# Hybrid encoder with experts: six pairs of split tiles with a set lead, splits ahead of all other work, and down rows in groups of four, four and three

## The chip, the cores and the metric

The kernel runs on one core of a Trainium2 chip. The metric is the device time of one launch in microseconds (us); the comparison is between the kernel before and the kernel with the change.

## What is computed

Two pre-RMSNorm residual layers on 256 tokens of width 1024, then a final RMSNorm, all in float32. Layer 0 is a bidirectional gated linear attention mixer and a dense SwiGLU; layer 1 is a banded attention with ALiBi and sinks, and then eight SwiGLU experts of which each token uses two. The part that the change is mostly about is

```
def swiglu(h, w_gate, w_up, w_down):
    return (silu(h @ w_gate) * (h @ w_up)) @ w_down      # 1024 -> 2816 -> 1024

logits = t @ router;  top_val, top_idx = top_k(logits, 2);  top_w = softmax(top_val)
for e in range(8):
    out += combine[:, e:e+1] * swiglu(t, w_gate[e], w_up[e], w_down[e])
```

The weights of one expert are 3 x 1024 x 2816 floats, 34.6 MB; the eight experts have 277 MB of the 341 MB that the kernel reads.

## The kernel before, in words

**Splits.** Products are made to near-float32 precision on float32r operands: each operand is the sum of a high part (rounded to float32r) and a low part. For a weight tile, ScalarE (ACT) writes `hi = copy(raw)` (line 174) and VectorE (DVE) writes `lo = raw - hi` (line 175). With both operands split a product takes three matmuls (`mm3`, lines 221 to 223: high with high, high with low, low with high). An expert of *kind 3* works so, on up to 128 gathered tokens. An expert of *kind 2* holds at most 64 tokens, so the high and the low part of the tokens sit side by side in the 128 columns of one operand, and two matmuls do (lines 1157 and 1158: one with `hi`, one with `lo` of the weights). The eight experts run in the order kind 3, 2, 3, 2, 3, 2, 3, 2; those after the first are sorted by token count, so that their weights are addressed by a register.

**The weight stream.** One object, `Weights`, carries all weights of the kernel in one list. `pump` starts loads into free raw slots from the SP queue; `split` makes the next `hi` and `lo` pair; `take` splits until `ahead` pairs beyond the one wanted are there and hands over one. Before the change a raw slot is 3072 floats a partition, one load fills it, and it is split as two tiles of up to 1536 floats; a slot is free when its second tile has been split. There are four raw slots at first, six after the first mixer and seven in the expert layer. The pairs come from a pool of three, and `ahead` is 1.

**As it is.** Of each kind 2 expert, four of the 48 tiles are not split (`AS_IS`, loads 1, 13, 17 and 20, the second half of each): TensorE (PE) takes the raw float32 tile itself (line 1155).

**One expert.** Gate and up each go in two halves of 11 column chunks; a half is eight tiles of 128 rows x 1408 columns, spread over three PSUM banks of 512, 512 and 384 columns (`UP` = 4, 4 and 3 chunks). After the eighth tile the banks are taken out (kind 2: ACT copies; kind 3: ACT Silu for gate, a DVE product for up). `turn_over` turns three such groups at a time to `hth` (and `htl`), hidden units on partitions, in the gate steps of the second half and at the first three down steps. Down goes in eight steps of three chunks of 128 rows (the last of one), each a pair of tiles of 512 columns, into two banks. At the fourth down step of a kind 3 expert the tokens of the next two experts are gathered (`after`, lines 1092 to 1116). The four `put` products of an expert, with their DVE additions to `h` (line 1230), run in the up steps of the next one.

**Order.** The program text gives a rank, and a list scheduler with a timeline model puts each engine's instructions into one queue; each engine runs its queue in order and waits at semaphores.

Of the kernel before, what the change touches and what calls it, by code (L numbers as in the profile page):

```python
# [11 lines left out]
F32 = mybir.dt.float32  # L12
# [6 lines left out]
P = 128  # L19
# [18 lines left out]
NQ = 16  # L38
# [13 lines left out]
WIDE = (3, 3, 3, 3, 3, 3, 3, 1)  # L52
# [8 lines left out]
AS_IS = (1, 13, 17, 20)  # L61
# [7 lines left out]
RAW = 3072  # L69
N_A, N_B, N_C = 4, 2, 1  # L70
# [8 lines left out]
def by_rows(w, r0, n, c0, c1, cut):  # L79

    return (w, r0, n, c0, c1), [(slice(k, min(k + cut, n)), slice(0, c1 - c0)) for k in range(0, n, cut)]


def by_cols(w, r0, n, c0, cuts):

    at = [sum(cuts[:i]) for i in range(len(cuts) + 1)]
    return (w, r0, n, c0, c0 + at[-1]), [(slice(0, n), slice(i, j)) for i, j in zip(at, at[1:])]


def plan_columns(w, c0, n=4):  # L90

    return [by_rows(w, k * P, n, c0, c0 + 512, 2) for k in range(0, KC, n)]


def plan_down(wd, c, cuts):

    loads = []
    f = 0
    for i in range(0, len(cuts), 2):
        n = sum(cuts[i : i + 2])  # L100
        loads.append(by_rows(wd, f * P, n, c * HALF, (c + 1) * HALF, cuts[i]))
        f += n
    return loads


def plan_dense(wg, wu, wd):


    loads = []
    f0 = 0  # L110
    for n_f in BLOCKS:
        for w in (wg, wu):
            for k in range(0, KC, 4):
                loads.append(by_cols(w, k * P, 4, f0 * P, (3 * P, (n_f - 3) * P)))
        f0 += n_f
    return loads + plan_down(wd, 0, DOWN[0]) + plan_down(wd, 1, DOWN[0])


def plan_expert(wg, wu, wd, last=False):


    loads = []
    for f0 in (0, FH):
        for w in (wg, wu):
            loads += [by_rows(w, k * P, 2, f0 * P, (f0 + FH) * P, 1) for k in range(0, KC, 2)]
    if last:
        return loads + plan_down(wd, 0, DOWN[0]) + plan_down(wd, 1, DOWN[1])
    f = 0
    for n in WIDE:
        loads.append(by_cols(wd, f * P, n, 0, (HALF, HALF)))  # L130
        f += n
    return loads


class Weights:
# [3 lines left out]

    def __init__(self, nc, split_pool, plan, slots, ahead=1, as_is=()):  # L140
        self.as_is, self.used = as_is, None
        self.nc, self.pool, self.plan, self.slots, self.ahead = nc, split_pool, plan, deque(slots), ahead
        self.loaded = deque()
        self.ready = deque()
        self.next = 0
        self.pump()

    def pump(self):
        while self.slots and self.next < len(self.plan):
            (w, *at), cuts = self.plan[self.next]  # L150
            src = rows(w if isinstance(w, bass.AP) else w(), *at)
            slot = self.slots.popleft()
            raw = slot.tile([P, RAW], F32, name="raw")
            v = self.view(raw, src.shape[1], src.shape[2])
            self.nc.sync.dma_start(v, src)
            for i, (a, b) in enumerate(cuts):
                as_is = (self.next, i) in self.as_is
                self.loaded.append((v[:, a, b], slot if i == len(cuts) - 1 else None, as_is))
            self.next += 1

    def view(self, t, n1, n2):
        return t[:, : n1 * n2].rearrange("p (a b) -> p a b", a=n1)

    def split(self):
        nc = self.nc
        v, slot, as_is = self.loaded.popleft()
        if as_is:
            self.ready.append((v, None))
            self.used = slot
            return  # L170
        n1, n2 = v.shape[1], v.shape[2]
        hi = self.view(self.pool.tile([P, SUB], F32R, name="hi"), n1, n2)
        lo = self.view(self.pool.tile([P, SUB], F32R, name="lo"), n1, n2)
        nc.scalar.activation(hi, v, AF.Copy)  # L174
        nc.vector.tensor_sub(lo, v, hi.bitcast(F32))  # L175
        self.ready.append((hi, lo))
        self.free(slot)

    def free(self, slot):
        if slot:  # L180
            self.slots.append(slot)
            self.pump()

    def done(self):

        slot, self.used = self.used, None
        self.free(slot)
# [5 lines left out]
    def take(self, n1, n2):  # L193
# [3 lines left out]
        assert list(wh.shape[1:]) == [n1, n2], (wh.shape, n1, n2)  # L197
        return wh, wl


@with_exitstack
def hybrid_encoder(ctx: ExitStack, tc: tile.TileContext, a: dict, out: bass.AP):
# [43 lines left out]
    for c0 in (0, KW, 2 * KW, 2 * KW + 512, 2 * KW + VW, 2 * KW + VW + 512):  # L246
        plan += plan_columns(w_in, c0, 4 if c0 else 2)
# [3 lines left out]
    plan += [by_rows(w_qkv, 0, KC, c0, c0 + 256, 4) for c0 in range(0, NQ * HD, 256)]  # L251
# [18 lines left out]
    as_is = set()  # L270
    for s in range(1, NE):
        if KINDS[s] == 2:
            as_is |= {(len(plan) + i, 1) for i in AS_IS}
        plan += plan_expert(*[expert_weights(n, s) for n in moe_w], s == NE - 1)
    weights = Weights(nc, split_p, plan, [raw_a] * 2, as_is=as_is)
# [752 lines left out]
    def moe_layer(x, cst):  # L1028
        with tc.tile_pool(name="moe", bufs=1) as g:
# [109 lines left out]
            def expert(src, kind, xe, weight, between=None, late=(), last=None):  # L1139
# [11 lines left out]
                def mm(ps, ah, al, bh, bl, start, stop):  # L1151
                    if kind == 3:
                        mm3(ps, ah, al, bh, bl, start, stop)
                    elif bl is None:
                        nc.tensor.matmul(ps, lhsT=ah.bitcast(F32), rhs=bh, start=start, stop=stop)  # L1155
# [30 lines left out]
                for f0 in (0, FH):  # L1186
                    ga = g.tile([P, FH * P], F32, name="gate")
                    up_ = g.tile([P, FH * P], F32, name="up") if kind == 2 else None
                    for m in ("g", "u"):
                        banks = [mm_bank() for _ in UP]  # L1190
                        for k in range(KC):
                            wh, wl = src.take(1, FH * P)
                            for (c, n), b in zip(UP, banks):
                                cs = slice(c * P, (c + n) * P)
                                b = b[:, : n * P]
                                mm(b, chunk(xeh, k), chunk(xel, k), wh[:, 0, cs], wl and wl[:, 0, cs], k == 0, k == KC - 1)
                                if k < KC - 1:
                                    continue
                                if kind == 2:
                                    nc.scalar.copy((ga if m == "g" else up_)[:, cs], b)  # L1200
                                elif m == "g":
                                    nc.scalar.activation(ga[:, cs], b, AF.Silu, scale=back[1])
                                else:
                                    nc.vector.tensor_mul(ga[:, cs], ga[:, cs], b)
                                if m == "u":
                                    todo.append((c, n, f0 + c, ga, up_))
                            if not wl:
                                src.done()
                            if not back:
                                back.extend(rest())  # L1210
                            elif todo and m == "g" and k in (1, 3, 5):
                                turn_over(*todo.popleft())
                            elif late and m == "u" and k in (1, 3, 5, 6):
                                late.popleft()()
# [34 lines left out]

                def down(c, b, f, n):  # L1250
                    wh, wl = src.take(n, HALF)
                    for j in range(n):
                        mm(b, chunk(hth, f + j), chunk(htl, f + j), wh[:, j, :], wl and wl[:, j, :], f + j == 0, f + j == FC - 1)
                    if not wl:
                        src.done()
# [16 lines left out]
                f = 0  # L1272
                for n in WIDE:
# [5 lines left out]
                    f += n  # L1279
# [82 lines left out]
            with tc.If(n_most > CAP):  # L1362
                with tc.For_i(0, NE, 1) as e:
# [6 lines left out]
                    puts, _ = expert(Weights(nc, split_p, plan_expert(*w), [raw_a] * N_A), 3, xe[0], wt)  # L1370
# [50 lines left out]
    raw_b = ctx.enter_context(tc.tile_pool(name="raw_b", bufs=N_B))  # L1421
    weights.slots += [raw_b] * N_B
    weights.pump()
# [5 lines left out]
    raw_c = ctx.enter_context(tc.tile_pool(name="raw_c", bufs=N_C))  # L1429
    weights.slots += [raw_c] * N_C  # L1430
    weights.pump()
# [32 lines left out]
```

## Time and profile before

| | |
|---|---|
| three runs | 1230.92, 1230.09, 1230.82 us, median 1230.82 us |
| profiled execution | 1229.29 us, its span 1227.5 us, mean granted PE clock 0.985 |
| busy in the span | PE 1162.9, PEld (weight loads of PE) 984.9, DVE 967.3, ACT 817.8, POOL 94.4 us |
| `lo` on DVE (line 175) | 469 instructions, 728.9 us |
| `hi` on ACT (line 174) | 469 instructions, 619.5 us |
| read from HBM | 341.19 MB |

Busy times are sums of recorded durations. Matmuls overlap, so a PE that is busy all the time isn't at its peak; the chain of waits shows how far apart their ends are. In time the span is: the first mixer to about 143 us, dense SwiGLU to about 340 us, attention to about 440 us, routing to about 461 us, then the experts, whose stages on PE begin at 560.78 us (kind 2), 644.2 (3), 747.93 (2), 832.5 (3), 935.92 (2), 1020.52 (3) and 1123.74 us (2, the last).

### The profile page before, as it was taken

The page shows a single profiled execution, that of the slowest core. Times are in us where ns is not written, and L with a number is a line of the kernel's source. Part 1 is how long each engine was busy: PE and PEld are TensorE (multiplying, and loading weights), DVE is VectorE, ACT ScalarE, POOL GpSimd, SP SyncE. Part 2 cuts the span into 40 slices and gives each one's busy share as a digit, 9 for nine tenths or more (in the row PEclk, how much of TensorE's full clock was granted, in tenths as well). Part 3 has the DMA queues.
Part 4 walks back from the last instruction along what each step waited for, and adds up shares of the span by engine and source line. Part 5 has one row for each costly group of instructions (what it writes and reads, how often), then busy time and mean ns, then how long its engine had stood idle before and what let it go on. Part 6 is the DMA issues. An engine that isn't in the chain of part 4 may idle for free.

```text
span 1227.5 us, 17018 instructions
## 1 busy us (share of the span) xinstructions
PE 1162.9 (95%) x6384; PEld 984.9 (80%) x6384; DVE 967.3 (79%) x1120; ACT 817.8 (67%) x982; POOL 94.4 (8%) x248
## 2 busy tenths in 40 slices
PE   7989999999988989999999999999999999999994
PEld 7879899998888778887878887877887877887872
DVE  5786765564488667898989888988988988987986
ACT  4653544444468647777877777877777877776874
POOL 2000200000058320000000000000000000000003
PEclk9999999999999979999999999999999999999998
DMA  8342764554442147989999988999988999998981
GB/s 281 119 157 86 269 222 151 191 201 158 132 170 96 61 176 271 365 309 344 422 405 393 362 310 326 422 384 400 365 323 313 422 396 406 349 358 292 412 333 37
DMA packets 95281, 343.41 MB, mean 280 GB/s; under 512 B 6404, under 2 KB 10678, under 8 KB 95192
## 3 DMA queue, kind: packets, MB, share of 16 engines
q1 hardware_dynamic: 92400, 340.81, 74.0%
q10 hardware_dynamic: 2648, 0.92, 0.3%
q8 instruction: 52, 0.85, 0.3%
q0 software_dynamic: 144, 0.52, 0.1%
q14 instruction: 37, 0.30, 0.1%
HBM read 341.19 MB, written 1.05 MB: 279 GB/s over the span
## 4 chain that ended last, share of the span: by engine, by line
PE 75%; DVE 11%; ACT 6%; issue 4%; DMA 2%; POOL 2%; ACTq 0%; DVEq 0%; POOLq 0%
PE mm L222 17%; PE mm L223 16%; PE mm L221 16%; DVE lo L175 7%; PE mm L1158 7%; PE mm L1157 6%; PE mm L1155 3%; PE tr L1176 3%; ACT hi L174 3%; PE mm L1224 1%; PE tr L1105 1%; DMA sink_raw<-in_swa_sinks_dram 1%; ACT p L900 1%; DVE y L1248 1%; PE tr L1167 1%
## 5 line engine op out<-in xcount | busy, mean ns | idle before, releaser
L175 DVE TENSOR_TENSOR lo<-raw,hi 128x1408 fp32r<-128x1408 f32 (+2 forms) x469 | 728.9, 1582 | 165.5 <-ACT hi L174 163.9
L174 ACT ACTIVATE hi<-raw 128x1408 fp32r<-128x1408 f32 (+2 forms) x469 | 619.5, 1342 | 304.8 <-PE mm L223 168.5
L221 PE MATMUL mm<-xh,hi 128*128 128x256 f32 x560 | 156.3, 286 | 4.8 <-ACT hi L174 3.8
L222 PE MATMUL mm<-xl,hi 128*128 128x256 f32 x560 | 157.8, 285 | 0.9 <-DVE xl L374 0.9
L223 PE MATMUL mm<-xh,lo 128*128 128x256 f32 x560 | 156.1, 284 | 0.0
L222 PE MATMUL mm<-lo,xeh 128*128 128x512 f32 (+1 forms) x384 | 145.4, 379 | 3.8 <-DVE lo L175 3.6
L223 PE MATMUL mm<-hi,xel 128*128 128x512 f32 (+1 forms) x384 | 144.0, 375 | 0.0
L221 PEld LDWEIGHTS mm<-xh,hi 128*128 128x128 f32 x560 | 105.9, 192 | 6.6 <-ACT hi L174 4.9
L1158 PE MATMUL mm<-lo,xeh 128*128 128x512 f32 x360 | 100.5, 389 | 9.7 <-DVE lo L175 9.6
L222 PEld LDWEIGHTS mm<-xl,hi 128*128 128x128 f32 x560 | 106.6, 191 | 1.5 <-DVE xl L374 1.1
L222 PE MATMUL mm<-lo,hth 128*128 128x512 f32 x264 | 105.0, 398 | 2.2 <-DVE lo L175 2.2
L223 PEld LDWEIGHTS mm<-xh,lo 128*128 128x128 f32 x560 | 105.9, 191 | 0.5 <-issue 0.3
L223 PE MATMUL mm<-hi,htl 128*128 128x512 f32 x264 | 104.4, 395 | 0.0
L221 PE MATMUL mm<-hi,hth 128*128 128x512 f32 x264 | 104.3, 401 | 0.0
L221 PE MATMUL mm<-hi,xeh 128*128 128x512 f32 (+1 forms) x384 | 103.8, 377 | 0.1
L1157 PE MATMUL mm<-hi,xeh 128*128 128x512 f32 x360 | 98.7, 385 | 1.0 <-ACT hi L174 0.8
L222 PEld LDWEIGHTS mm<-lo,xeh 128*128 128x128 f32 x384 | 72.5, 189 | 22.4 <-DVE lo L175 7.2
L1158 PEld LDWEIGHTS mm<-lo,xeh 128*128 128x128 f32 x360 | 63.2, 188 | 29.7 <-DVE lo L175 20.9
L223 PEld LDWEIGHTS mm<-hi,xel 128*128 128x128 f32 x384 | 72.4, 189 | 11.4
L1157 PEld LDWEIGHTS mm<-hi,xeh 128*128 128x128 f32 x360 | 65.9, 188 | 15.1 <-ACT hi L174 3.1
L221 PEld LDWEIGHTS mm<-hi,xeh 128*128 128x128 f32 x384 | 70.5, 189 | 7.6 <-ACT hi L174 1.5
L1158 PE MATMUL mm<-lo,hth 128*128 128x512 f32 x152 | 61.2, 411 | 3.3 <-DVE lo L175 3.2
(305 smaller groups left out, 1557.1 us busy)
## 6 DMA issues: line engine op xcount, KB each, us to landing
raw<-in_moe_w_gate_dram SPq DMA_DIRECT2D x64, 1408.0 KB, 8.7
raw<-in_moe_w_up_dram SPq DMA_DIRECT2D x64, 1408.0 KB, 8.6
raw<-in_moe_w_down_dram SPq DMA_DIRECT2D x53, 1536.0 KB, 9.4
raw<-in_gla_in_proj_dram SPq DMA_DIRECT2D x10, 1024.0 KB, 5.1
raw<-in_dense_w_gate_dram SPq DMA_DIRECT2D x4, 1536.0 KB, 6.6
raw<-in_dense_w_up_dram SPq DMA_DIRECT2D x4, 1536.0 KB, 9.5
raw<-in_dense_w_down_dram SPq DMA_DIRECT2D x4, 1536.0 KB, 7.4
raw<-in_swa_qkv_proj_dram SPq DMA_DIRECT2D x6, 1024.0 KB, 4.8
```

The lines of the kernel that those rows point to most:

```text
L174: nc.scalar.activation(hi, v, AF.Copy)
L175: nc.vector.tensor_sub(lo, v, hi.bitcast(F32))
L221: nc.tensor.matmul(ps, lhsT=ah, rhs=bh, start=start, stop=False)
L222: nc.tensor.matmul(ps, lhsT=ah, rhs=bl, start=False, stop=False)
L223: nc.tensor.matmul(ps, lhsT=al, rhs=bh, start=False, stop=stop)
L900: nc.scalar.activation(p[:, t, :], p[:, t, :], AF.Exp, scale=float(SLOPES[hd]), bias=m[:, 2 + t : 3 + t], accum_out=den[:, t : t + 1])
L1105: i = nc.tensor.matmul(o, lhsT=part[:, t, cs], rhs=oh[:, t, :w], start=t == 0 and part is x.hh, stop=t == NT - 1 and part is x.hl)
L1155: nc.tensor.matmul(ps, lhsT=ah.bitcast(F32), rhs=bh, start=start, stop=stop)
L1157: nc.tensor.matmul(ps, lhsT=ah, rhs=bh, start=start, stop=False)
L1158: nc.tensor.matmul(ps, lhsT=ah, rhs=bl, start=False, stop=stop)
L1167: nc.tensor.transpose(pt[:, i * P : (i + 1) * P], ga[:, (c + i) * P : (c + i + 1) * P], ident)
L1176: nc.tensor.matmul(pt[:, o : o + FEW], lhsT=src_[:, (c + i) * P : (c + i + 1) * P], rhs=by, start=True, stop=True)
```

## The change

- A raw slot is 1536 floats a partition, one load fills it with one tile. There are eight slots all along; the pools `raw_b` and `raw_c` are gone. In the expert layer the slots hold 8 x 6 KB a partition, before 7 x 12 KB.
- From the expert layer on the pairs come in turn from two pools of three, six pairs in all.
- No tile is used as it is; all 48 of a kind 2 expert are split.
- `ahead` is set from a table at every step: it goes 2, 2, 3, 4, 5 through the five parts of a kind 3 expert and 5, 4, 3, 3, 2 through those of a kind 2 expert.
- All ACT and DVE instructions of a gate, up or down step other than splits (taking out the banks, `turn_over`, gather, `put`) are queued behind the last `hi` and the last `lo` that had been issued when the step began (`behind`). The down steps of the last expert have no such order.
- Down of all experts but the last: six groups of 4, 4, 3, 4, 4, 3 row chunks. In a group of n chunks partition p holds rows p*n to p*n+n-1, one run of n*4 KB in memory, cut into tiles of 1536 (for n = 4 the last has 1024); before, a row chunk was 128 rows, one on each partition. To fit, the gate and up banks are read with a step of n floats (`b.rearrange("p (q j) -> p j q")`). `turn_over` still comes at the end of the first three groups, the gather at the end of the fourth.
- Outside the experts the loads are cut to single tiles too (dense gate and up 384 columns a row instead of 768).

```
+AHEAD = {
+    (3, 0, "g"): 2, (3, 0, "u"): 2, (3, FH, "g"): 3, (3, FH, "u"): 4, (3, "d"): 5,
+    (2, 0, "g"): 5, (2, 0, "u"): 4, (2, FH, "g"): 3, (2, FH, "u"): 3, (2, "d"): 2,
+}
-RAW = 3072
-N_A, N_B, N_C = 4, 2, 1
+N_A = 8
...
+def in_a_row(w, r0, n, c0, c1):
+    return w, lambda v: v[r0 : r0 + n * P, :].rearrange("(p r) c -> p (r c)", r=n)[:, c0:c1]
...
+def down_steps():
+    f = 0
+    for _ in range(2):
+        for _, n in UP:
+            for c in range(0, n * D, SUB):
+                yield f, n, c, min(c + SUB, n * D)
+            f += n
...
     def split(self):
-        v, slot, as_is = self.loaded.popleft()
-        if as_is:
-            self.ready.append((v, None))
-            self.used = slot
-            return
...
+        pool = self.pools[self.n_split % len(self.pools)]
+        self.n_split += 1
+        hi = self.view(pool.tile([P, SUB], F32R, name="hi"), v)
+        lo = self.view(pool.tile([P, SUB], F32R, name="lo"), v)
+        i = nc.scalar.activation(hi, v, AF.Copy)
+        j = nc.vector.tensor_sub(lo, v, hi.bitcast(F32))
+        self.last = i.ins, j.ins
         self.ready.append((hi, lo))
-        self.free(slot)
+        self.slots.append(slot)
+        self.pump()
...
+    @contextmanager
+    def behind(self, tc):
+        with ExitStack() as order:
+            for i in self.last:
+                order.enter_context(tc.issue_after(i))
+            yield
...
                         for k in range(KC):
+                            src.ahead = AHEAD[kind, f0, m]
                             wh, wl = src.take(1, FH * P)
...
+                            with src.behind(tc):
+                                for (c, n), b in zip(UP, banks):
...
+                                    to = (ga if m == "g" or kind == 3 else up_)[:, cs]
+                                    if not last:
+                                        to = to.rearrange("p (j q) -> p j q", j=n)
+                                        b = b.rearrange("p (q j) -> p j q", j=n)
...
-                for n in WIDE:
-                    for c, b in enumerate(banks):
-                        down(c, b, f, n)
-                        if f + n == FC:
-                            done(c, b)
-                    mid(0)
-                    f += n
+                for f0, n, c0, c1 in down_steps():
+                    wh, wl = src.take(c1 - c0)
+                    with src.behind(tc):
+                        for i in range(c0, c1, HALF):
+                            f, c = f0 + i // D, i // HALF % 2
+                            ws = slice(i - c0, i - c0 + HALF)
+                            mm(banks[c], chunk(hth, f), chunk(htl, f), wh[:, ws], wl[:, ws], f == 0, f == FC - 1)
+                            if f == FC - 1:
+                                done(c, banks[c])
+                        if c1 == n * D:
+                            mid(0)
...
-    raw_c = ctx.enter_context(tc.tile_pool(name="raw_c", bufs=N_C))
-    weights.slots += [raw_c] * N_C
-    weights.pump()
+    weights.pools = [split_p, ctx.enter_context(tc.tile_pool(name="split_b", bufs=3))]
+    weights.n_split = 0
```

## Rows read from the trace of the kernel before

**Rows 1.** Busy time of each engine over the span (the page's first part).

```profile
PE 1162.9 (95%) x6384; PEld 984.9 (80%) x6384; DVE 967.3 (79%) x1120; ACT 817.8 (67%) x982; POOL 94.4 (8%) x248
```

**Rows 2.** Busy time by stretch: stages of kind 2, kind 2 and kind 3.

```profile
core 0: us, PE busy (x) PEld busy (x) DVE busy (x) ACT busy (x) POOL busy (x), PEclk, DMA share, GB/s
560.78:644.20 83.42, 80.92 (x383) 63.40 (x384) 76.56 (x68) 67.81 (x72) 0.00 (x0) 1.00 0.98 397
...
747.93:832.50 84.57, 81.59 (x383) 62.98 (x383) 76.68 (x68) 67.81 (x72) 0.00 (x0) 1.00 0.98 389
832.50:935.92 103.42, 101.42 (x490) 85.21 (x489) 90.06 (x85) 75.48 (x72) 0.00 (x0) 1.00 0.92 351
```

**Rows 3.** The same view for line 175 (`lo`) alone: DVE busy and count.

```profile
747.93:832.50 84.57, 68.72 (x45) 1.00 0.98 389
832.50:935.92 103.42, 76.52 (x49) 1.00 0.92 351
```

**Rows 4.** Waits, 747.93 to 832.5 us: total us, times, longest.

```profile
ACT hi L174 <- PE mm L1157: 11.7, 9, 2.5
DVE lo L175 <- ACT hi L174: 9.6, 8, 2.1
```

**Rows 5.** Waits, 832.5 to 935.92 us.

```profile
ACT hi L174 <- PE mm L223: 24.2, 34, 1.8
DVE lo L175 <- ACT hi L174: 12.2, 17, 2.2
```

**Rows 6.** Chain of waits, 745 to 790 us: start, us, what.

```profile
754.76 2.36 PE mm L1155 x6
...
761.00 1.28 PE mm L1157 x6
...
769.48 0.93 PE mm L1224 x4
...
783.91 1.28 PE tr L1176 x12
```

**Rows 7.** Chain of waits, 806 to 846 us.

```profile
809.39 2.57 PE mm L1155 x6
...
811.97 0.23 PE mm L1157
...
841.86 0.64 PE mm L221 x3
```

**Rows 8.** Chain of waits, 895 to 925 us.

```profile
909.26 1.76 PE tr L1105 x16
```

**Rows 9.** Timeline of DVE in two kind 2 stretches: start, us, instruction.

```profile
752.19 6.22 DVE L175 TENSOR_TENSOR lo<-raw,hi 128x1408 fp32r<-128x1408 f32 x4
...
818.43 6.76 DVE L175 TENSOR_TENSOR lo<-raw,hi 128x1536 fp32r<-128x1536 f32 x4
```

**Rows 10.** Timeline of PE where a kind 2 expert begins.

```profile
747.93 0.91 PE L1157 MATMUL mm<-hi,xeh 128*128 128x512 f32 x3 [0.30 <-ACT hi L174]
749.59 0.91 PE L1158 MATMUL mm<-lo,xeh 128*128 128x512 f32 x3 [0.75 <-DVE lo L175]
```

**Rows 11.** DVE groups by form, 832.5 to 935.92 us.

```profile
L1204 DVE TENSOR_TENSOR gate<-gate,mm 128x512 f32<-128x512 f32 x4 | 2.6, 681 | 1.8 <-PE mm L223 1.8
```

**Rows 12.** ACT groups by form, 747.93 to 832.5 us.

```profile
L1200 ACT COPY up<-mm 128x512 f32<-128x512 f32 x4 | 2.2, 590 | 1.0 <-PE mm L1158 1.0
```

**Rows 13.** DMA, 760 to 800 us: totals, and issues with median us to landing.

```profile
DMA packets 3563, 16.89 MB, mean 422 GB/s; under 512 B 176, under 2 KB 176, under 8 KB 3560
...
raw<-in_moe_w_up_dram SPq DMA_DIRECT2D x4, 1408.0 KB, 9.0
```

**Rows 14.** Issue times on SP, 760 to 790 us: ns min, median, max.

```profile
L155 SPq DMA_DIRECT2D raw<-in_moe_w_up_dram x4: 372/372/373, 767.7 to 778.9; - x4
```

**Rows 15.** Busy time by stretch: the start and the middle of dense gate and up.

```profile
140.00:160.00 20.00, 17.68 (x134) 16.53 (x134) 14.27 (x25) 9.48 (x16) 10.09 (x86) 1.00 0.92 342
200.00:220.00 20.00, 20.00 (x170) 20.00 (x170) 11.98 (x13) 7.72 (x9) 0.00 (x0) 1.00 0.53 186
```

More of the change, by code (lines that the diff above doesn't have):

```diff
@@ L76, in rows, with chunks, plan_columns @@
     return w[r0 : r0 + n * P, c0:c1].rearrange("(k p) c -> p k c", p=P)
[L79 to L92, printed above, removed]
-def plan_down(wd, c, cuts):
[L97 to L101, printed above, removed]
-        f += n
-    return loads
+def chunks(w, r0, n, c0, c1):
+    return w, lambda v: rows(v, r0, n, c0, c1)
+def in_a_row(w, r0, n, c0, c1):
+    return w, lambda v: v[r0 : r0 + n * P, :].rearrange("(p r) c -> p (r c)", r=n)[:, c0:c1]
+def plan_columns(w, c0):
+    return [chunks(w, k * P, 2, c0, c0 + 512) for k in range(0, KC, 2)]
+def plan_down(wd, c, cuts):
+    at = [sum(cuts[:i]) for i in range(len(cuts))]
+    return [chunks(wd, f * P, n, c * HALF, (c + 1) * HALF) for f, n in zip(at, cuts)]
 def plan_dense(wg, wu, wd):
@@ L113, in plan_dense @@
             for k in range(0, KC, 4):
-                loads.append(by_cols(w, k * P, 4, f0 * P, (3 * P, (n_f - 3) * P)))
+                for c in range(0, n_f, 3):
+                    loads.append(chunks(w, k * P, 4, (f0 + c) * P, (f0 + min(c + 3, n_f)) * P))
         f0 += n_f
     return loads + plan_down(wd, 0, DOWN[0]) + plan_down(wd, 1, DOWN[0])
+def down_steps():
[5 more added lines that the diff above has]
+            f += n
 def plan_expert(wg, wu, wd, last=False):
@@ L124, in plan_expert, with __init__ @@
         for w in (wg, wu):
[L125 removed]
+            loads += [chunks(w, k * P, 1, f0 * P, (f0 + FH) * P) for k in range(KC)]
     if last:
         return loads + plan_down(wd, 0, DOWN[0]) + plan_down(wd, 1, DOWN[1])
[L128 to L132 removed]
+    return loads + [in_a_row(wd, f * P, n, c0, c1) for f, n, c0, c1 in down_steps()]
 class Weights:
[L140 to L142 removed]
+    def __init__(self, nc, split_pools, plan, slots, ahead=1):
+        self.nc, self.pools, self.plan, self.slots, self.ahead = nc, split_pools, plan, deque(slots), ahead
         self.loaded = deque()
         self.ready = deque()
[L145 removed]
+        self.next = self.n_split = 0
         self.pump()
@@ L149, in pump, with view @@
         while self.slots and self.next < len(self.plan):
-            (w, *at), cuts = self.plan[self.next]
-            src = rows(w if isinstance(w, bass.AP) else w(), *at)
+            w, pick = self.plan[self.next]
+            src = pick(w if isinstance(w, bass.AP) else w())
             slot = self.slots.popleft()
-            raw = slot.tile([P, RAW], F32, name="raw")
-            v = self.view(raw, src.shape[1], src.shape[2])
+            raw = slot.tile([P, SUB], F32, name="raw")
+            v = self.view(raw, src)
             self.nc.sync.dma_start(v, src)
-            for i, (a, b) in enumerate(cuts):
-                as_is = (self.next, i) in self.as_is
-                self.loaded.append((v[:, a, b], slot if i == len(cuts) - 1 else None, as_is))
+            self.loaded.append((v, slot))
             self.next += 1
-    def view(self, t, n1, n2):
+    def view(self, t, like):
+        if len(like.shape) == 2:
+            return t[:, : like.shape[1]]
+        n1, n2 = like.shape[1], like.shape[2]
         return t[:, : n1 * n2].rearrange("p (a b) -> p a b", a=n1)
@@ L165, in split @@
         nc = self.nc
-        v, slot, as_is = self.loaded.popleft()
-        if as_is:
-            self.ready.append((v, None))
-            self.used = slot
-            return
[L171 to L175, printed above, removed]
-        self.ready.append((hi, lo))
-        self.free(slot)
[L179 to L187, printed above, removed]
+        v, slot = self.loaded.popleft()
+        pool = self.pools[self.n_split % len(self.pools)]
[5 more added lines that the diff above has]
+        self.last = i.ins, j.ins
+        self.ready.append((hi, lo))
+        self.slots.append(slot)
+        self.pump()
     def fill(self, n):
@@ L250, in hybrid_encoder @@
     plan += plan_columns(w_qkv, NQ * HD)
-    plan += [by_rows(w_qkv, 0, KC, c0, c0 + 256, 4) for c0 in range(0, NQ * HD, 256)]
+    plan += [chunks(w_qkv, k * P, 4, c0, c0 + 256) for c0 in range(0, NQ * HD, 256) for k in (0, 4)]
     plan += plan_columns(w_so, 0) + plan_columns(w_so, HALF)
@@ L1248, in done @@
                     nc.vector.tensor_sub(y[0][:, c, 1], bank, y[0][:, c, 0].bitcast(F32))
+                src.ahead = AHEAD[kind, "d"]
                 def down(c, b, f, n):
@@ L1252, in down @@
                     for j in range(n):
[L1253 to L1255 removed]
+                        mm(b, chunk(hth, f + j), chunk(htl, f + j), wh[:, j, :], wl[:, j, :], f + j == 0, f + j == FC - 1)
                 if last:
```

66 lines of the change are left out of this document (25 added, 41 removed).

## The prediction

> **What bounds the kernel now.** I read the engine totals first [rows 1]: PE is busy 95% of the span, but matmul records overlap, so this says little; VectorE at 79% is an average over unlike stages. So the next view is busy time by stretch, cut where PE goes from one expert to the next [rows 2]. A kind 2 stage takes 84.57 us and VectorE is busy for 76.68 of them; a kind 3 stage takes 103.42 us, VectorE 90.06. Nearly all of that is `lo` [rows 3]. The first kind 2 stage, 83.42 us with VectorE busy 76.56, repeats the pattern.
>
> What PE itself needs comes from the chain of waits, where successive starts give the real pitch. A kind 2 gate or up tile is six matmuls in 1.28 us, a kind 3 tile three times 0.64 = 1.92, a 512 column down product 0.23, a `put` product 0.23, one turning product 1.28 / 12 = 0.107, a tile taken as it is 2.36 (gate, up) or 2.57 us (down) [rows 6, 7]. Kind 2 before: 30 x 1.28 + 2 x 2.36 + 76 x 0.23 + 2 x 2.57 + 88 x 0.107 + 8 x 0.23 = 77.0 us, so PE loses 7.6 of 84.6. Kind 3: 32 x 1.92 + 132 x 0.23 + 22 x 0.107 + 2 x 1.76 for the gather [rows 8] + 1.9 = 99.6, so it loses 3.8 of 103.4. So kind 3 is bound by PE, and kind 2 has two engines within 8 us of its length.
>
> Why VectorE idles 7.9 us in a kind 2 stage: `lo` waits for `hi`, and `hi` waits for PE to free one of three pairs [rows 4]. In kind 3 the same chain makes most of 13.4 us of idle time (`lo` waits 17 times for `hi`, `hi` 34 times for PE) [rows 5]: there VectorE could run ahead, and has no pair to write. So a kind 2 expert starts with no lead: PE waits 0.75 us for the very first `lo` [rows 10].
>
> **The change part by part.**
>
> *No tile as it is.* Each kind 2 expert gets four more splits. Back to back a `lo` of 1408 takes 6.22 / 4 = 1.56 us, one of 1536 6.76 / 4 = 1.69 [rows 9]: 2 x 1.56 + 2 x 1.69 = 6.5 us more on VectorE, 83.2 us a stage. ScalarE gets fewer than 6 us more on 67.81, and has the room. PE gives back 4.5 us: 32 x 1.28 + 88 x 0.23 + 9.4 + 1.9 = 72.5 us. Taken alone this makes kind 2 a VectorE stage that is only 1.4 us shorter than now with no idle time at all.
>
> *Six pairs and the lead.* A lead of L tiles at the start of a kind 2 stage takes 1.56 L us off VectorE's work there and puts it into the kind 3 stage before. The table allows L = 5, now L is 0. Kind 3 has 13.4 us for it; 5 tiles take 7.8, and then 97.9 of about 102 us are busy. I take L = 4, because the gather and its products fall into the last down steps and compete for VectorE there. Kind 2 then needs 83.2 - 6.2 = 77.0 us of VectorE, above PE's 72.5. The idle part of 7.9 us, mostly waits for a pair, should shrink with six pairs; I take 2.8, with 0 and 7.9 as ends. Kind 2: 79.8 us, that is 4.8 less. By the ends: 75.4 (L = 5, no idle) to 91.1 (L = 0, idle as now).
>
> *Kind 3.* Of the 3.8 us that PE loses, the wait at the end of the stage goes (there is a lead now), the waits of the first tiles stay, since a kind 2 stage still ends with VectorE last. I take 1.5 us less; ends 0 and 3.8.
>
> *Splits ahead of everything else.* Taking out banks, `turn_over`, gather and `put` now stand behind up to five splits on both engines. Where PE is late (kind 3) these splits are done early and nobody waits. Where VectorE is late (kind 2), a `put` addition or a `turn_over` product comes up to four splits, 6.2 us, later. The queue behind is more splits, so VectorE doesn't idle, and PE, which has 72.5 us of work in some 80, can lose it; the first down step that needs a late group comes 4 to 5 steps after its `turn_over`. I take 0; the ends are in the idle range above. The gather moves from after 12 of 22 row chunks to after 15, which leaves 7 x 6 x 0.23 = 9.7 us of down products for it (before 13.8) and its own 3.5; its VectorE work is small next to the five splits beside it. Cost 0, up to 3 us if its last products come late.
>
> *Loads.* The same bytes in twice as many transfers. Issuing takes 0.37 us on SP [rows 14], against some 1.8 us a tile. Now about 9.0 us from issue to landing at 422 GB/s are 3.8 MB, 2.6 transfers of 1.44 MB, in flight [rows 13]; that is 5.3 of the new ones, and eight slots leave 2.7 tiles that wait raw, beside the pairs. At the forecast a pair of experts (69.2 MB) takes 181.7 us, 381 GB/s, under the 422 that the queue has shown over 40 us. I take 0; for the other end see the rivals. Down runs get longer (6 KB, before 4 KB), also 0. On the Trainium skill: "DMA: Bandwidth & Descriptors" (Bandwidth, Measured) wants 1 MiB a transfer for 75% of peak, and these are under it; by its 2 us of fixed time and 436 GB/s one 0.72 MB transfer alone would run at an estimated 198 GB/s and the experts would take twice as long. The trace shows several in flight at once, which hides that fixed time, so I don't use it as a term.
>
> *Banks read with a step.* No row has such a read. Bounds: as now, or twice as long. Kind 3 has six DVE products of about 0.62 us (512 columns 0.68 in [rows 11]), kind 2 twelve ACT copies of about 0.55 (0.59 in [rows 12]): at most 3.8 us more DVE a kind 3 stage and 6.6 ACT a kind 2 stage. ACT has that room; on DVE it would eat into the lead. I take 0, as for the reads in rows. The Trainium skill ("PSUM — Partial Sum Buffer", Specifications) speaks against it: PSUM lines are 8 bytes and a pattern that isn't contiguous slows matmuls; it says nothing of reads by the other two engines, and no run here shows it.
>
> *Before the experts.* Dense gate and up keep PE busy in every microsecond at 186 GB/s [rows 15], so smaller slots and shorter runs have cover; if it went, the 2.3 us that PE is idle at 140 to 160 us show the size. There is less loaded in advance when the experts begin (8 tiles, before 14), but the first expert is kind 3. I take 0, ends -3 and +3.
>
> **Sum.** Four kind 2 stages x 4.8 + three kind 3 stages after one of kind 2 x 1.5 = 23.7 us; the first kind 3 stage is as long as PE needs already. Span 1227.5 - 23.7 = 1203.8, execution 1205.6 (1.8 us lie outside the span), and as the median of runs is 1.5 us above the profiled execution, 1207 us.
>
> **The rivals.**
>
> 1. *VectorE follows without idling.* L = 5, no idle time in kind 2 (75.4 us, -9.2) and kind 3 at PE's 99.6 plus 1.3 (-2.5): 4 x 9.2 + 3 x 2.5 = 44, 1187 us. For it: stretches of [rows 9] already run back to back. Against: two engines at over 95% at once, one fed by the other.
> 2. *The lead isn't built, so the four splits are paid (slower).* A kind 2 stage is 83.2 - 1.56 L + idle; it is longer than 84.6 when L is under (idle - 1.4) / 1.56: at 5 us of idle time, under 2.3. With L = 1 and 5 idle it is 86.6, +2.0 x 4 = 8: 1239 us; with L = 0 and idle as now +26: 1257. For it: evictions and gather in kind 3 now stand in VectorE's queue and wait there for PE, and idle time in bits of at most 2.2 us [rows 5] may not be usable. Against: those bits are waits for a pair, and now there are pairs.
> 3. *Loads bound it.* With 2.7 tiles in store (4.7 us) each hiccup of VectorE leaves the DMA without slots. If a pair then gets only the 351 GB/s of a kind 3 stage now, it takes 197 us, 9 more than now, x 4: 1267 us. For it: in kind 2 the DMA share is 0.98 [rows 2]. Against: in kind 3 it is low because slots come late, not because transfers are slow. By the skill's 1 MiB rule this would be the likely one.
> 4. *Reads with a step cost double.* The lead loses 3.8 us: kind 2 gains 1.0 instead of 4.8, so 15 us of the 24 go: 1222 us. The skill's PSUM sentence would make this one.
> 5. *It cancels.* Lead and idle time gain just what the splits cost: 1231 us.
>
> **How the numbers follow.** What a measurement of this kernel tells from no change is about 0.2%, 2.5 us. Forecast (1195 to 1219) 0.50; rival 1 (below) 0.17; rival 4 0.07; rival 5 0.08; rival 2 0.12; rival 3 0.06. Faster 0.50 + 0.17 + 0.07 = 0.74, same 0.08, slower 0.18. The range takes in rival 1 to its value and rival 2 nearly to its first: 1187 to 1237, leaving out some 7% below and 11% above.
>
> **What would show it.** Per expert 48 `lo` instead of 44 in kind 2, no line for raw tiles in matmuls; kind 2 stages near 80 us with VectorE busy at least 76 and the waits of `hi` for PE smaller; kind 3 stages near 102 us with VectorE busy over 95; no wait of PE for the first `lo` of a kind 2 expert. DMA about 381 GB/s over the experts. The forecast is wrong if kind 2 stages stay above 84 us, if ScalarE's `hi` starts to wait for loads, if the products at the banks last longer than the rows here, or if a kind 3 stage gets longer than 103 us.

## The result, and the profile after

The changed kernel takes 1216.72 us (median of 4 runs, 1213.25 to 1219.08), the kernel before 1230.57 us on the same chip: ratio 0.9883, 95% interval 0.9864 to 0.9902, or 13.9 us less. The forecast was 1207 us: right in sign and inside its range, and 9.7 us too low. The profiled execution has a span of 1215.4 us (before 1227.5).

Line numbers moved: `hi` is line 172, `lo` 173, kind 2 products are 1150 and 1151, the gather's products 1100, its evictions 1107 (ACT) and 1111 (DVE), bank evictions 1200 to 1204. The engine totals of after, which answer to [rows 1]:

```profile
PE 1151.2 (95%) x6384; PEld 994.5 (82%) x6384; DVE 982.8 (81%) x1136; ACT 830.1 (68%) x1000; POOL 95.0 (8%) x248
```

PE's busy time fell by 11.7 us, VectorE's rose by 15.5, with sixteen more splits (`lo` is now x485). Busy time by stage of after (kind 2, 3, 2, 3, and the last kind 2 stage to the end of the span), as in [rows 2]: window, length, then busy us and count of PE, PEld, DVE, ACT and POOL, granted clock, DMA share, GB/s.

```profile
562.70:643.04 80.34, 78.12 (x406) 65.57 (x404) 78.94 (x77) 70.13 (x78) 0.00 (x0) 1.00 0.99 386
643.04:742.12 99.08, 98.44 (x467) 83.17 (x466) 89.41 (x77) 72.17 (x67) 0.00 (x0) 1.00 1.00 392
742.12:826.80 84.68, 80.85 (x404) 66.70 (x405) 81.57 (x80) 73.30 (x81) 0.00 (x0) 0.98 0.94 361
826.80:925.90 99.10, 98.44 (x468) 83.16 (x466) 89.43 (x77) 72.22 (x67) 0.00 (x0) 1.00 0.99 391
...
1109.27:1215.40 106.13, 84.93 (x406) 67.41 (x406) 89.75 (x94) 76.34 (x94) 8.79 (x4) 0.91 0.72 267
```

Kind 3 lost 4.3 us (103.4 to 99.1), where 1.5 were forecast. Kind 2 lost nothing (84.57 to 84.68), where 4.8 were forecast; only the first kind 2 stage is at 80.3. A pair of stages (742.12 to 925.90) takes 183.78 us, VectorE busy for 171.0, so 12.8 idle; before it was 188.0 and 166.7, so 21.3 idle. On the span the 12.1 us are made up so: the experts reach their first kind 2 stage 1.9 us later, the three pairs give 7.7, 4.2 and 4.5, and the last stage takes 2.4 more (103.76 before).

The same view for `lo` alone, as in [rows 3], and then for the gather's DVE products (line 1111) and its PE products (line 1100) in the kind 2 stage:

```profile
742.12:826.80 84.68, 72.18 (x46) 0.98 0.94 361
826.80:925.90 99.10, 78.60 (x51) 1.00 0.99 391
```

```profile
742.12:826.80 84.68, 3.65 (x14) 0.98 0.94 361
```

```profile
742.12:826.80 84.68, 3.03 (x16) 2.82 (x16) 0.98 0.94 361
```

A kind 3 expert has 48 tiles and its stage splits 51 (edges counted): a lead of about three tiles is handed over. And half of the gather, which before lay wholly in the kind 3 stage, now runs in the kind 2 stage: 14 of its 16 DVE products, 16 of its 32 PE products. PE's half of it, 1.76 us by [rows 8], is the larger part of the 2.8 us that kind 3 gains beyond the forecast; the 3.65 us of VectorE are part of why kind 2 gains nothing.

Waits of after in that kind 2 stage (as in [rows 4]) and in the kind 3 stage behind it (as in [rows 5]): engine, line, what it waited for, us, times, longest.

```profile
PEld mm L1151 <- DVE lo L173: 6.1, 11, 1.5
...
DVE lo L173 <- ACT hi L172: 3.1, 4, 1.0
...
PE mm L1151 <- DVE lo L173: 1.9, 4, 1.1
ACT gate L1200 <- PE mm L1151: 1.5, 1, 1.5
...
ACT up L1200 <- PE mm L1151: 0.7, 1, 0.7
```

```profile
ACT hth L1162 <- PE tr L1160: 9.6, 4, 5.5
ACT xeh L1107 <- PE tr L1100: 5.5, 2, 5.3
DVE lo L173 <- ACT hi L172: 5.5, 3, 2.6
...
ACT hi L172 <- PE mm L221: 5.0, 10, 0.7
DVE xel L1111 <- ACT xeh L1107: 4.0, 1, 4.0
```

`hi` waiting for a pair fell from 24.2 to 5.0 us in kind 3 and is gone in kind 2. In its place ScalarE stands at evictions that wait for PE, at the gather 5.3 us in one piece, and VectorE behind it 4.0. In the kind 3 stage itself PE loses nothing by it (busy 98.44 of 99.10 us); what it uses up is lead. PE timeline of after, the gather's first product and the one where PE waits in the next stage:

```profile
739.69 0.25 PE L1100 MATMUL tr<-oh,hh 128*128 128x192 f32 x1
...
745.60 0.50 PE L1100 MATMUL tr<-oh,hh 128*128 128x192 f32 x1 [1.95 <-DVE xeh L1111]
```

Reads with a step, DVE at 826.8 to 925.9 us and ACT at 742.12 to 826.8 us by form (as in [rows 11, 12]):

```profile
L1204 DVE TENSOR_TENSOR gate<-gate,mm 128x512 f32<-128x512 f32 x4 | 2.6, 680 | 0.0
```

```profile
L1200 ACT COPY up<-mm 128x512 f32<-128x512 f32 x4 | 2.1, 587 | 0.7 <-PE mm L1151 0.7
```

680 ns against 681, 587 against 590 for 512 columns, read with a step of four floats. The banks of 384 columns, with a step of three, take 546 ns against 546 on VectorE (line 1204) and 502 against 498 on ScalarE (`up`, line 1200). The step costs nothing.

### The profile page after: what moved, and what is told of

It is laid out like the page before. It is cut to its first block, busy times and chain, and to the rows that moved or that the text cites. A ratio compares the mean times of both kernels' runs of the same rounds, so it can differ in the third digit from the quotient of the medians.

```text
span 1215.4 us, 18063 instructions
## 1 busy us (share of the span) xinstructions
PE 1151.2 (95%) x6384; PEld 994.5 (82%) x6384; DVE 982.8 (81%) x1136; ACT 830.1 (68%) x1000; POOL 95.0 (8%) x248
## 4 chain that ended last, share of the span: by engine, by line
PE 75%; DVE 9%; issue 6%; ACT 6%; POOL 1%; DMA 1%; SPq 0%; ACTq 0%; DVEq 0%; POOLq 0%
PE mm L220 18%; PE mm L221 18%; PE mm L219 18%; PE mm L1151 7%; PE mm L1150 6%; DVE lo L173 5%; ACT hi L172 3%; PE tr L1169 2%; PE tr L1100 1%; PE mm L1222 1%; PE tr L1160 1%; ACT p L895 1%; DMA raw<-in_moe_w_down_dram 1%; POOL q L869 1%; PE mm L1100 1%
## 5 line engine op out<-in xcount | busy, mean ns | idle before, releaser
L173 DVE TENSOR_TENSOR lo<-raw,hi 128x1408 fp32r<-128x1408 f32 (+2 forms) x485 | 750.5, 1583 | 129.3 <-ACT hi L172 128.8
L172 ACT ACTIVATE hi<-raw 128x1408 fp32r<-128x1408 f32 (+2 forms) x485 | 631.1, 1344 | 195.6 <-PE mm L221 103.3
L220 PE MATMUL mm<-lo,xeh 128*128 128x512 f32 (+1 forms) x384 | 145.8, 380 | 0.4
L1151 PE MATMUL mm<-lo,xeh 128*128 128x512 f32 (+1 forms) x384 | 121.2, 391 | 1.1 <-DVE lo L173 1.1
L1150 PE MATMUL mm<-hi,xeh 128*128 128x512 f32 (+1 forms) x384 | 119.1, 384 | 1.1 <-ACT xeh L1107 1.0
L219 PE MATMUL mm<-hi,xeh 128*128 128x512 f32 (+1 forms) x384 | 113.9, 377 | 0.0
L220 PE MATMUL mm<-lo,hth 128*128 128x512 f32 x264 | 104.8, 397 | 0.0
L219 PE MATMUL mm<-hi,hth 128*128 128x512 f32 x264 | 96.1, 396 | 0.0
L220 PEld LDWEIGHTS mm<-lo,xeh 128*128 128x128 f32 x384 | 72.8, 190 | 16.4 <-DVE lo L173 1.5
L1151 PEld LDWEIGHTS mm<-lo,xeh 128*128 128x128 f32 x384 | 69.6, 192 | 18.1 <-DVE lo L173 8.5
L1150 PEld LDWEIGHTS mm<-hi,xeh 128*128 128x128 f32 x384 | 72.6, 192 | 13.3 <-ACT xeh L1107 1.3
L219 PEld LDWEIGHTS mm<-hi,xeh 128*128 128x128 f32 x384 | 71.8, 190 | 7.7
L1151 PE MATMUL mm<-lo,hth 128*128 128x512 f32 x176 | 65.0, 414 | 9.2 <-DVE lo L173 9.1
```

What stands on the lines that cost most here:

```text
L172: i = nc.scalar.activation(hi, v, AF.Copy)
L173: j = nc.vector.tensor_sub(lo, v, hi.bitcast(F32))
L220: nc.tensor.matmul(ps, lhsT=ah, rhs=bl, start=False, stop=False)
```

## The experiments

Ratios are to the kernel before on the same chip, with 95% intervals.

**Where the gather stands.** In the first two kernels it moves: ahead of the first `turn_over` of down, or out of the order behind the splits.

```
                 def mid(c):
+                    if between and not ahead:
+                        ahead.append(between())
                     if todo:
                         turn_over(*todo.popleft())
-                    elif between and not ahead:
-                        ahead.append(between())
```

> The gather of a kind 3 expert comes at the end of the first group of down rows instead of the fourth; all else as in the changed kernel (1216.7 us). Theory A: the changed kernel loses 4.2 us at each of the last three passages from kind 3 to kind 2 (its pairs of stages take 183.6 us, the one whose gather is half in time 179.4), because the gather's matmuls stand after the last down product. Then 3 x 4.2 = 13 us go: about 1204 us, with the first kind 2 tile waiting for no gather and the granted clock at 1.00 there. Theory B: VectorE's work as a whole bounds a pair of stages, and the place of the gather only moves idle time about: 1215 to 1219 us.

e1: 1232.37 us, 1.0024 (1.0013 to 1.0035), 16 us more than the changed kernel; theory A is out. By stage, and the waits of the kind 3 stage:

```profile
837.40:947.66 110.26, 104.46 (x484) 88.37 (x482) 95.47 (x92) 77.53 (x74) 0.00 (x0) 0.95 0.90 343
947.66:1025.06 77.40, 75.85 (x389) 63.95 (x388) 76.32 (x65) 68.02 (x73) 0.00 (x0) 1.00 1.01 411
```

```profile
ACT xeh L1107 <- PE tr L1100: 7.3, 3, 5.6
...
PE tr L1100 <- DVE xeh L1111: 4.2, 1, 4.2
```

Kind 2 now has the lead and takes 77.4 us, less than I had forecast, but kind 3 pays 11 us: the stand moved with the gather, and now PE stands too.

```
-                    elif between and not ahead:
-                        ahead.append(between())
...
                         if c1 == n * D:
                             mid(0)
+                    if c1 == n * D and between and not turning and not ahead:
+                        ahead.append(between())
```

> The gather stays at the end of the fourth group of down rows but isn't queued behind the newest splits. If it is the order behind the splits that makes it late (theory A1), this does most of what the earlier place does: about 1206 us. If it is the place, after 15 of 22 row chunks (theory A2): 1213 to 1217 us. Theory B: 1215 to 1219.

e2: 1215.53 us, 0.9888 (0.9874 to 0.9901), as the change itself; A2 and B both allow it. The kind 2 stage:

```profile
741.73:826.09 84.36, 80.58 (x398) 63.68 (x396) 82.11 (x77) 72.07 (x79) 0.00 (x0) 1.00 0.99 384
```

PE no longer waits for the gather there and its clock stays at 1.00, but the stage is only 0.3 us shorter, and PE's idle time in it is 3.8 us, as in after. So neither the order at the gather nor PE's clock there is what the forecast missed.

**The table of leads, and the raw tiles.**

```
-AHEAD = {(3, 0, "g"): 2, (3, 0, "u"): 2, (3, FH, "g"): 3, (3, FH, "u"): 4, (3, "d"): 5, ...}
+AHEAD = {(3, 0, "g"): 2, (3, 0, "u"): 2, (3, FH, "g"): 2, (3, FH, "u"): 2, (3, "d"): 2, ...}   # all 2
```

> The table of leads is 2 everywhere, with six pairs still. If the set lead is what carries VectorE's work into the kind 3 stages (three tiles of 1.56 us a kind 2 stage), 4 x 4.7 = 19 us come back: about 1235 us, with 48 or 49 of the low parts in a kind 2 stage in place of 46. If the six pairs alone do it, because the scheduler draws splits forward into free pairs anyway: 1215 to 1220 us.

e3: 1211.91 us, 0.9849 (0.9833 to 0.9866), below both expectations; a set lead of up to five is no gain, and rather a loss (the intervals just overlap). VectorE does the same work (171.1 us a pair) in 182.1 us instead of 183.8 (the view's sum over both stages, 742.02 to 924.16 us):

```profile
sum 182.14, PE 178.43 PEld 148.10 DVE 171.12 ACT 144.37 POOL 0.00; mean PE 89.21 PEld 74.05 DVE 85.56 ACT 72.19 POOL 0.00
```

```
+AS_IS = (3, 27, 35, 41)        # of the 48 tiles of a kind 2 expert
...
+        if as_is:
+            self.ready.append((v, None))
+            self.held.append(slot)
+            return
...
+                    elif bl is None:
+                        nc.tensor.matmul(ps, lhsT=ah.bitcast(F32), rhs=bh, start=start, stop=stop)
```

> Four tiles of each kind 2 expert are used as they are again, with the six pairs, the leads and the order of the changed kernel. By the sum, VectorE has 6.5 us less and PE 4.5 us more in a kind 2 stage. If VectorE bounds these stages (busy 81.6 of 84.7 us), they get up to 4 us shorter until PE bounds them: about 1204 us. If PE's loss at the passages bounds them, the 4.5 us come on top: 1225 to 1235 us.

e4: 1209.04 us, 0.983 (0.9817 to 0.9842), nearer to the first expectation: splitting the four tiles costs some 6.5 us of what the rest gains. Over the pair from 739.47 us PE is now busy for 180.0 of 181.1 us, VectorE for 165.4:

```profile
sum 181.14, PE 179.99 PEld 149.22 DVE 165.35 ACT 141.05 POOL 0.00; mean PE 89.99 PEld 74.61 DVE 82.68 ACT 70.52 POOL 0.00
```

From here on *theory C*: room for six pairs makes the gain, and in the changed kernel VectorE's total bounds a pair of stages; the written order matters little.

**One part at a time.**

```
-    weights.pools = [split_p, ctx.enter_context(tc.tile_pool(name="split_b", bufs=3))]
+    weights.pools = [split_p]                       # and AHEAD all 2, as in e3
```

> Three pairs of split tiles through the expert layer, as in the kernel before, with a lead of two everywhere; load sizes, the order behind the splits, down groups and the four further split tiles per kind 2 expert stay as changed. Theory C (room for splits is what gains, less the price of splitting the four tiles, some 6 us over the program by e4): 1231 to 1240 us, kind 2 stages 86 us or longer. Rival D (the written order behind the splits is what gains, the room for them is not needed): 1209 to 1214 us, as e3 with its lead of two.

e5: 1226.0 us, 0.997 (0.9958 to 0.9981), between the two theories: against e3 room is worth 14 us, but without it there is still a gain of 0.3%. The wait for a pair is back in kind 3:

```profile
ACT hi L169 <- PE mm L218: 21.6, 34, 1.6
DVE lo L170 <- ACT hi L169: 9.2, 19, 1.7
```

```
     def behind(self, tc):
         with ExitStack() as order:
-            for i in self.last:
-                order.enter_context(tc.issue_after(i))
             yield
```

> The changed kernel without the written order: other work is no longer queued behind the splits, all else stays. Theory C: the order gives under 3 us either way, since room and VectorE's total decide: 1213 to 1220 us. Rival D (the order is what gains): 1226 to 1232 us.

e6: 1232.39 us, 1.0019 (1.0003 to 1.0034). This is where theory C, and my prediction, fell: without the order nothing is left of the gain. By stage, then the waits of the kind 2 stage, then ACT and DVE in it:

```profile
746.81:833.62 86.81, 82.14 (x383) 61.38 (x382) 79.44 (x70) 71.38 (x75) 0.00 (x0) 1.00 0.95 363
833.62:935.21 101.59, 100.96 (x489) 85.52 (x488) 92.25 (x86) 73.24 (x72) 0.00 (x0) 1.00 0.98 372
```

```profile
PEld mm L1149 <- DVE lo L173: 17.2, 33, 1.2
ACT up L1198 <- PE mm L1149: 7.2, 2, 4.7
DVE lo L173 <- ACT hi L172: 5.4, 4, 1.8
PE mm L1149 <- DVE lo L173: 4.7, 12, 0.8
ACT gate L1198 <- PE mm L1149: 3.3, 2, 2.1
...
DVE y L1244 <- ACT y L1243: 1.6, 1, 1.6
...
DVE h L1226 <- PE mm L1220: 1.2, 2, 0.6
```

```profile
759.08 10.27 ACT L172 ACTIVATE hi<-raw 128x1408 fp32r<-128x1408 f32 x8
774.03 1.07 ACT L1198 COPY up<-mm 128x512 f32<-128x512 f32 x2 [4.68 <-PE mm L1149]
...
776.42 1.62 DVE L173 TENSOR_TENSOR lo<-raw,hi 128x1408 fp32r<-128x1408 f32 x1 [1.44 <-ACT hi L172]
```

After the gate banks ScalarE does eight splits, and then its queue has the eviction of `up`, whose products PE has not finished: it stands for 4.68 us with further splits queued behind that eviction. VectorE runs out of `hi` in turn, here for 1.44 us. In the stage it waits 5.4 us for `hi` (3.1 in after), and 2.8 us at its own share of the other work, the taking out of down and the `put` additions (lines 1244 and 1226). PE's products and weight loads wait 21.9 us for `lo`, both added up (8.0 in after). With the order the stands of ScalarE at gate and up are 2.2 us instead of 10.5. VectorE's work per pair is nearly the same (171.7 and 171.0 us); its idle time is 16.7 instead of 12.8. The lead is not what is lost: the two stages of e6 have 46 and 51 `lo`, as in after, and the gather is back in the kind 3 stage. That the order is what gains is shown by leaving it out; that it gains by the stands is read from these waits, since no run moved the evictions alone.

```
-N_A = 8
+N_A = 6
```

> Six raw buffers for loads in place of eight, all else as changed. Theory C: loads lead by several tiles and bound nothing: 1214 to 1219 us, waits of hi on a load under 2 us per stage. Rival E (the loads are close to a bound since the raw space went to split tiles): 1224 us or more, hi waiting on loads 2 us or more per stage.

e7: 1227.24 us, 0.9978 (0.9961 to 0.9995); rival E, some 10 us. `hi` now waits for loads, here in the kind 3 stage from 648.49 us, where in after the waits for loads are under 1 us a stage:

```profile
ACT hi L172 <- DMA raw<-in_moe_w_down_dram: 2.8, 5, 1.5
ACT hi L172 <- DMA raw<-in_moe_w_gate_dram: 2.7, 5, 1.1
```

e8 is e4 with the table of e3:

```
+AS_IS = (3, 27, 35, 41)        # as in e4
+AHEAD = {...}                  # all 2, as in e3
```

> Six pairs, four raw tiles per kind 2 expert used unsplit (as in the kernel before), lead of two everywhere: e3 and e4 in one. Theory C (VectorE's total bounds a pair; with the lead of two the pile-up at the gather is smaller as well, both gains partly add): 1203 to 1208 us. Rival F (both undo the same wait; once VectorE has four tiles less per pair of experts the lead no longer matters): 1209 us, within 1.5 us of e4.

e8: 1209.42 us, 0.9839 (0.9826 to 0.9853), e4 again: with the four tiles off VectorE the table no longer matters. PE is busy 98 and 100% of its stages:

```profile
739.49:822.96 83.47, 82.10 (x406) 65.91 (x405) 77.25 (x74) 67.77 (x75) 0.00 (x0) 1.00 0.98 378
822.96:921.07 98.11, 98.11 (x468) 83.19 (x467) 88.63 (x79) 72.95 (x69) 0.00 (x0) 1.00 0.97 386
```

**What the gather costs, and the order and the room beside unsplit tiles.**

```
             def after(s):
...
+                if s in (2, 4):
+                    return dict(zip(pair, first_got))
```

> The gathers for experts 3 to 6 are left out: these experts use the rows gathered for experts 1 and 2 again (the last expert's gather stays). Of the changed kernel's three full pairs of stages two lose their gather. Theory C (a gather costs its own VectorE work, some 5.8 us, and the lead that ScalarE burns standing at the gather's eviction, 4 to 5 us of VectorE idling): some 9 us for each of the two, 1197 to 1201 us, and the kind 2 stage behind a kind 3 stage without a gather 80 us or less. Rival H (own work alone, no lead is lost): 5.8 us each, 1204 to 1206 us. Rival I (the gather lies beside other work): 1211 us or more.

e9: 1202.88 us, 0.9769 (0.9754 to 0.9784): 13.8 us less than the change, 6.9 for each gather, between theory C and rival H. A pair of stages without it:

```profile
639.03:736.32 97.29, 97.15 (x458) 82.04 (x457) 90.27 (x72) 74.22 (x66) 0.00 (x0) 1.00 0.99 391
736.32:814.83 78.51, 76.68 (x383) 62.80 (x382) 76.44 (x65) 68.24 (x73) 0.00 (x0) 1.00 1.00 398
```

175.8 us against 183.8: VectorE has 4.3 us less to do (166.7) and idles 9.1 instead of 12.8, so of these 8.0 us 4.3 are the gather's own work there and 3.7 the lead that it burns, roughly: the profiled execution of e9, 1196.78 us, is 6 us below its median.

```
# e8, and
-            for i in self.last:
-                order.enter_context(tc.issue_after(i))
```

> e8 (six pairs, four raw tiles per kind 2 expert unsplit, lead of two) without the written order behind the splits. Theory J (the order pays by keeping ScalarE from standing at evictions ahead of splits, which matters only as far as VectorE is short; with four tiles less it has about 6 us per pair in hand of the 4 to 5 that the missing order cost per pair in e6): 1209 to 1214 us. Rival D (the order is worth its 16 us whatever VectorE has to do): 1222 to 1226 us.

e10: 1227.42 us, 0.9979 (0.9968 to 0.999). Theory J missed: the order is worth its 1.4% (17 us) here too, though VectorE had 6 us a pair less to do. Its work per pair is that of e8 (165.9 us), and it idles 21.6 us where e8 idles 15.7. The sum over the pair from 743.86 us, and the stand of ScalarE at `up` in its kind 2 stage, as in e6 (`gate` has 4.8 us more):

```profile
sum 187.53, PE 183.53 PEld 148.09 DVE 165.91 ACT 140.02 POOL 0.00; mean PE 91.76 PEld 74.04 DVE 82.95 ACT 70.01 POOL 0.00
```

```profile
ACT up L1215 <- PE mm L1166: 8.2, 2, 4.7
```

```
-AS_IS = (3, 27, 35, 41)        # e8
+AS_IS = (27, 41)
```

> e8 with two raw tiles per kind 2 expert unsplit in place of four. Theory J (in e4 and e8 TensorE is the bound, busy 98 to 99% of both stages, and an unsplit tile costs it some 0.6 us; with two tiles VectorE and TensorE are about level): 1206 to 1209 us. Rival K (VectorE binds again as soon as tiles go back to it): halfway to e3, 1210 to 1212 us.

e11: 1207.5 us, 0.9823 (0.9809 to 0.9836), the fastest of the kernels that compute the whole function, though its interval overlaps those of e4 and e8. In kind 2 PE is busy 97% and VectorE 96%, so the two are level, and a pair takes 180.8 us:

```profile
739.58:822.05 82.47, 80.31 (x406) 65.58 (x405) 79.48 (x76) 69.96 (x77) 0.00 (x0) 1.00 0.98 382
822.05:920.37 98.32, 98.17 (x468) 83.16 (x467) 88.76 (x79) 72.88 (x69) 0.00 (x0) 1.00 0.98 385
```

```
# e8, and
+    weights.pools = [split_p]
```

> e8 with three pairs of split tiles in place of six: the written order, the smaller loads and the down groups of the change on the room and the unsplit tiles of the kernel before. Theory J (room pays as far as VectorE is short, as the order does): 1211 to 1216 us. Rival L (room is worth the 14 us between e5 and e3 whatever VectorE has to do): 1222 to 1225 us.

e12: 1215.33 us, 0.9884 (0.9869 to 0.9899): beside unsplit tiles room is worth 0.5%, not the 1.2% between e3 and e5. With no more room than before and the same four tiles unsplit, the order with the smaller loads, the down groups and a lead of two already gives what the whole change gives.

Together (lead of two, but for those marked t, which have the table):

| | order, six pairs | order, three pairs | no order, six pairs |
|---|---|---|---|
| every tile split | 0.9849; changed kernel (t) 0.9883 | 0.997 | 1.0019 (t) |
| four tiles unsplit | 0.9839; (t) 0.983 | 0.9884 | 0.9979 |

The kernel before is three pairs, four unsplit, no order, with a lead of one, larger loads and other down rows. Small loads and down groups were not run without the other parts, nor three pairs without the order.

## Why the prediction was right and wrong

- *Splits ahead of everything else: 0, up to 3 us lost.* This is the step that failed. I treated the order as a possible cost and gave its gain to the six pairs. It is the condition of nearly the whole gain: e6 and e10, with everything else of the change that they share, stand within 0.3% of before, 1.4% (some 17 us by the ratios) above their twins, the changed kernel and e8. The reason, as far as the waits show it, is the one I used the wrong way round in rival 2: an engine's queue stands at an eviction that waits for PE. I saw evictions queued behind splits as the danger; splits queued behind evictions are the worse case, since PE needs the splits. So the time lies in the range partly by luck: by the prediction's own signs it was wrong, as kind 2 stages stayed above 84 us (84.68, 84.60) and VectorE in kind 3 is busy for 89.4 us, not over 95.
- *Six pairs, a lead of 4, 2.8 us idle in kind 2.* The lead is about three tiles, the idle time 3.1 us (84.68 - 81.57). VectorE has 81.57 us to do in kind 2, where I had 77.0: 3.65 of the 4.6 are the gather's products. The pairs are not the condition that I took them for, as e12 has three and gives what the change gives; their worth hangs on how short VectorE is: 1.2% (e5 to e3) or 0.5% (e12 to e8).
- *No tile as it is: VectorE +6.5, PE -4.5 us.* Per pair VectorE has 5.6 us more than in e4, and the exchange loses 0.5% (6.5 us) beside the table of leads, and 0.1%, which the intervals don't tell from nothing, beside a lead of two. I had it as a step that makes kind 2 a VectorE stage, and that is so; that a better version keeps two or four raw tiles I had not drawn from it.
- *Kind 3: -1.5 us.* It was -4.3: 1.76 is half of the gather, which left the stage, so some 2.5 are waits of PE that went. *Gather: inside its room, 0 to 3 us.* The room of 9.7 us was not used: VectorE, which has splits ahead, writes the selection matrix (line 1087) by 732.8 us, but PE's queue has the first of its products at 739.69 us, behind the last down product, and ScalarE, whose queue has their eviction next and splits behind it, stands 5.3 us for them. In e6, without the order, all 16 VectorE products of the gather are in the kind 3 stage again. A pair together was forecast at -6.3 and gave -4.2 to -7.7, so pairs are 2.5 us short in all; that this is so little, with kind 2 at 0 in two of three for -4.8, and kind 3 at -4.3 for -1.5, is luck too.
- *The last stage: -4.8 us like the others.* It took 2.4 more, and with 7.2 us this is the largest term of the 11.6 us that the profiled span missed (the rest is 1.9 before the first kind 2 stage). VectorE has 89.75 us to do there, before 86.76: four splits more, 6.5, and 1.78 of its gather, less three tiles of lead, 4.7, make 3.6, and 3.0 were measured. Its down steps have no written order, and its idle time did not shrink (16.4 us, before 17.0). The granted clock over it was 0.91, before 0.94, and how much of the 2.4 us that is wasn't separated. That an order there would help was not run; with four tiles unsplit (e8) the stage takes 104.3 us.
- *Loads: 0.* Right, but near an edge: eight slots left 2.7 tiles in store by my sum, six would leave 0.7, and e7 shows the loads bind there. Rival 3 is out for eight.
- *Reads with a step: 0.* Right [rows 11, 12]; rival 4 is out.
- *Before the experts: 0.* PE's first product of the first expert starts at 462.9 us, before at 458.6, and 1.9 us of that are left at the first kind 2 stage. It goes with the six pairs: the eleven runs that have them start it at 460.8 to 464.1, the two with three pairs (e5, e12) at 457.8 and 457.9. ScalarE of after does four splits into the new room before it writes the second half of the router's operand `hT` (line 977), in e5 one, and PE's router products wait for that operand, 3.1 us in each of the eleven, 0.2 in e5, e12 and before. From the timelines of ScalarE and PE in after:

```profile
441.46 5.18 ACT L172 ACTIVATE hi<-raw 128x1408 fp32r<-128x1408 f32 x4 [1.48 <-PE mm L221]
...
447.05 3.58 PE L1037 MATMUL mm<-router,hT 128*128 128x8 f32 x16 [3.06 <-ACT hT L977]
```

- Rival 1 is out: a pair still has 12.8 us of VectorE idle time. Rival 2's kind 2 stage of 86.6 us was seen only where the order was taken away (86.81 in e6), and there by idle time, not by a lead that wasn't built. Rival 5 is out: the change is 1.2% faster.

What stays open: which of small loads and down groups carries anything by itself; which of the ordered work (taking out banks, `turn_over`, gather, `put`) the order gains by; whether the router's operand ahead of those splits would give the 3 us back; and why the table of leads costs VectorE idle time when all tiles are split.

## What to carry to other kernels

Where an engine both prepares operands for TensorE and takes out its results, look at the stages in which TensorE waits for operands, and there for the waits at an eviction with preparations queued behind it. More buffers without the order of the queue did little here (e10, 0.2%). The same room let preparations run ahead of work that TensorE needed sooner, the router's operand. Then see which engine is at its total: here leaving two of 48 tiles unsplit to TensorE gave some 0.3% (e11 against e3), the table of leads nothing. Price a moved step (the gather) in the stage it moves into as well as in the one that it leaves.

## What the runs showed of the hardware

Bank reads with a step of three or four floats take as long as reads in a row on both engines (512 columns, step of four: 680 and 681 ns, 587 and 590 ns; 384 columns, step of three: 546 and 546 ns, 502 and 498 ns). After PE's wait of 1.95 us at 745.60 us its 512 column products followed each other at 0.43 to 0.48 us, and at 0.23 us again some 4 us later, as the chain of waits of after shows below (start, us, what); the granted clock from 742.12 to 752.12 us was 0.83, so part of that stretch ran at 1.2 GHz in place of 2.4. e2, without that wait, had 1.00 over its stage and was no faster; VectorE was busy there for 82.1 of 84.4 us.

```profile
747.59 0.48 PE mm L1150
748.07 0.43 PE mm L1151
...
749.60 0.23 PE mm L1150
```

Two raw slots of 0.7 MB fewer cost 10 us, though the queue moved 355 GB/s over e7's kind 2 stage from 747.55 us and has shown 422 [rows 13].
